# One decoder layer in one program: the mLSTM denominators, with blocks of scores and weighted queries added on VectorE ahead of the product with the ones column

## The chip, the core and the metric

The kernel runs on one core of one Trainium2 chip. The metric is the device time of one execution in microseconds. Three runs of the kernel before gave 2320.81, 2321.09 and 2322.24 us; the median is 2321.09 us.

## What is computed

One layer of a hybrid decoder for 256 prompt tokens and 8 x 8 sample tokens, 320 tokens in all, in fp32. An input projection feeds two token mixers, an mLSTM (4 heads, key width 256, value width 512) and an HGRN2 (8 heads); their outputs are gated, projected, normalised, and followed by a feed-forward part. The change touches only the denominator of the mLSTM:

```python
        s = jnp.einsum('bhtk,bhsk->bhts', qc, kc) * d
        num = jnp.einsum('bhts,bhsv->bhtv', s, vc) + w_inter[..., None] * jnp.einsum('bhtk,bhkv->bhtv', qc, C)
        den = jnp.sum(s, axis=-1) + w_inter * jnp.einsum('bhtk,bhk->bht', qc, n)
        h = num / jnp.maximum(jnp.abs(den), jnp.exp(-m_t))[..., None]
```

`den` is, for each token, the sum of its row of scores, and for sample tokens also the weighted query times the normaliser state `n`.

## The kernel before

**Main products.** TensorE multiplies the 320 tokens by one 128-column tile of weights after another (`run_main`, lines 499 to 534). Each weight is held as a high and a low part in a rounded fp32 format (`wh`, `wl`, later `bb`), each activation as well (`xh`, `xl`), so that each 128 x 128 block takes three products: high by high, high by low, low by high. These are the rows with 128x320 on line 348, the helper through which nearly all products go. A weight half-tile (a unit, 128x1024) is loaded by a DMA into `wr` (line 496), ScalarE writes its high part (line 486, shown as line 342, ScalarE's helper), and VectorE subtracts to get the low part (line 488).

**Side work.** All else (mixers, gates, norms) is written as Python generators that a planner (`Sched`, lines 144 to 242) runs while the main products are emitted. After every block of three main products the planner is pumped: a generator's next operation is emitted if, by the planner's own estimate of each engine's time, its inputs will be ready by then. TensorE operations must by that estimate be ready 450 units of time (nanoseconds of the planner) ahead, and only some 900 units of them fit between two blocks. The result is one fixed order of instructions for each engine, with semaphore waits between engines.

**The mLSTM heads.** For each head `m_S` (line 905) makes scores: three blocks of score products are multiplied by decay factors into the tile `E`. Columns 0 to 127 are prompt tokens 0 to 127 against keys 0 to 127, columns 128 to 255 are tokens 128 to 255 against keys 0 to 127, columns 256 to 383 are tokens 128 to 255 against keys 128 to 255, and columns 384 to 511 (partitions 64 to 127) the sample tokens. ScalarE and VectorE then split `E` into high and low parts (lines 925 to 929) for the numerator's products. `m_num` (line 1056) makes numerators and denominators of the prompt tokens: a block of `E` as the stationary operand times a column of ones (`one`, in the tile `misc`) gives row sums in a PSUM bank (lines 1069 to 1071: one product for the first tile of tokens, two that accumulate for the second). `m_sample` (line 1128) does the sample tokens: it writes the weighted queries times `n` into two blocks of the tile `qn` (line 1141), and takes three accumulating products with the ones column, one with the sample block of `E` and two with `qn` (lines 1159 to 1161). Line 1163 copies the sum out of PSUM on VectorE.

So each head has six products with the ones column, 24 in all. In the profile they are the rows `bank<-misc,f` 128x1; being plain fp32, each is two passes, so the profile counts 48 and its timeline shows each as x2.

`E`, `qn` and the weighted queries are parts of the tiles that the profile calls `f`; `ra` are the rounded parts for numerators.

Of the kernel before, what the change touches and what calls it, by code (L numbers as in the profile page):

```python
# [13 lines left out]
ALU = mybir.AluOpType  # L14
# [230 lines left out]
def wait(*evs):  # L245
    return ("wait", evs)


def acq(pool, n=1):
    return ("acq", pool, n)  # L250
# [6 lines left out]
def post(ev):  # L257
    return ("set", ev)


def act(n, psum=False, ptr=0):
    return ((61 if psum else 112) + n) / 1.2 + 93 * ptr


def dve(n, psum=False, mode=1, ptr=0):
    return ((62 if psum else 66) + n / mode) / 0.96 + 55 * ptr
# [6 lines left out]
def pe_r(n):  # L273
    return max(108.0, n * 0.425)
# [8 lines left out]
def cap(ap, off, dims):  # L283
    return bass.AP(ap.tensor, ap.offset + off, [list(ap.ap[0])] + [list(x) for x in dims])


def by_row(ap, off, gap):

    return cap(ap, off, [[32, 4], [8, 2], [1, 8]] if gap else [[8, 4], [32, 2], [1, 8]])


def by_token(ap, off, gap):

    return cap(ap, off, [[8, 2], [32, 4], [1, 8]] if gap else [[32, 2], [8, 4], [1, 8]])
# [11 lines left out]
class Program:  # L306
# [598 lines left out]
    def m_S(self, h):  # L905
        v, m = self.nc.vector, self.mh[h]
        if h:
            yield wait(self.mh[h - 1]["S"])
        yield wait(*m["q"], *m["k"], m["E"])
        b = yield acq(self.sbank)  # L910
        qk = m["qk"]
        for lo, n, ks, qs in ((0, 256, 0, lambda c: qk[:, c, 0:256]), (256, 128, 128, lambda c: qk[:, c, 128:256]),
                              (384, 64, 192, lambda c: by_row(qk[:, c, :], 256, False))):
            for c in range(2):
                yield ("pe", pe_f(n), lambda: self.mm(
                    b[:, lo:lo + n], qk[:, 2 + c, ks:ks + 128], qs(c), start=c == 0, stop=c == 1))
        E, Es = m["eb"], m["Es"]
        yield ("dve", dve(384, True), lambda: v.tensor_tensor(E[:, 0:384], b[:, 0:384], E[:, 0:384], ALU.mult))
        yield ("dve", dve(64, True), lambda: v.tensor_tensor(Es, b[64:128, 384:448].rearrange("p (x r) -> p x r", x=4), Es, ALU.mult))
        yield rel(self.sbank, b)  # L920
        shl = yield acq(self.shl)
        m["shl"] = shl
        sh, sl, ss = shl
        f = lambda x: x.bitcast(F32)
        yield ("act", act(384), lambda: self.A(sh, E[:, 0:384]))
        yield ("act", act(128), lambda: self.A(ss[64:128, 0:128], E[64:128, 384:512]))
        yield ("dve", dve(384), lambda: v.tensor_tensor(sl, E[:, 0:384], f(sh), ALU.subtract))
        yield ("dve", dve(128), lambda: v.tensor_tensor(ss[64:128, 128:256], E[64:128, 384:512], f(ss[64:128, 0:128]), ALU.subtract))
        yield ("act", act(256), lambda: self.A(ss[0:64], f(ss[64:128])))
        yield post(m["S"])  # L930

    def m_V(self, h):
# [123 lines left out]
    def m_num(self, h):  # L1056
        v, m = self.nc.vector, self.mh[h]
        if h:
            yield wait(self.mh[h - 1]["N"])
        yield wait(m["S"], m["Vt"])  # L1060
        hb = yield acq(self.hb)
        m["hb"] = hb
        E = m["eb"]
        sh, sl, ss = m["shl"]
        vh, vl = m["vhl"][:, 0], m["vhl"][:, 1]
        db = yield acq(self.sbank)
        m["db"] = db
        one = self.one
        yield ("pe", 212, lambda: self.mm(db[:, 0:1], E[:, 0:128], one, start=True, stop=True))
        yield ("pe", 212, lambda: self.mm(db[:, 1:2], E[:, 128:256], one, start=True, stop=False))  # L1070
        yield ("pe", 212, lambda: self.mm(db[:, 1:2], E[:, 256:384], one, start=False, stop=True))
        for i in range(2):
            b = yield acq(self.sbank)
            jobs = [(c, s) for c, s in (((0, 0),), ((128, 0), (256, 1)))[i]]
            n = 0
            for c, s in jobs:
                for x, w in ((sh, vh), (sh, vl), (sl, vh)):
                    st, sp = n == 0, n == 3 * len(jobs) - 1
                    yield ("pe", pe_r(512), lambda: self.mm(b, x[:, c:c + 128], w[:, s, :], start=st, stop=sp))
                    n += 1  # L1080
            yield from self.ln_post(h, i, b, db[:, i:i + 1], hb[:, i, :], 128, True)
            yield rel(self.sbank, b)
        yield rel(self.sbank, db)
        yield post(m["N"])
# [43 lines left out]
    def m_sample(self, h):  # L1128
        nc, v, m = self.nc, self.nc.vector, self.mh[h]
        if h:  # L1130
            yield wait(self.mh[h - 1]["QW"])
        yield wait(*m["q"], m["bc_"], self.rows_ev)
        qk, bc = m["qk"], m["bc"]

        qz = yield acq(self.qz)
        qn = yield acq(self.qn)
        for c in range(2):
            qc = cap(qz, 256 * c, [[136, 2], [32, 4], [1, 8]])
            yield ("dve", dve(64), lambda: v.tensor_tensor(qc, by_token(qk[:, c, :], 256, False), by_token(bc, 640, False), ALU.mult))
            n4 = cap(self.n0[:, h, c, :], 0, [[4, 2], [1, 4], [0, 8]])  # L1140
            yield ("dve", dve(64), lambda: v.tensor_tensor(by_token(qn, 128 * c, True), qc, n4, ALU.mult))
        yield post(m["QW"])
        nb = yield acq(self.sbank)
        for k in range(2):
            yield wait(*m["parts"][8 * k:8 * k + 8])
            cbs = m["cbs"][8 * k:8 * k + 8]
            yield ("pe", PE_C, lambda: [self.mm(
                nb[32 * x:32 * x + 32, :], qz[:, 256 * c + 128 * k + 32 * x:256 * c + 128 * k + 32 * x + 32], cbs[4 * c + x],
                start=k == 0 and c == 0, stop=False, skip_group_check=True) for c in range(2) for x in range(4)])
            for c in range(2):  # L1150
                self.s.spawn(self.m_update(h, 8 * k + 4 * c, cbs[4 * c:4 * c + 4]), 3)
        yield rel(self.qz, qz)
        yield wait(m["S"], m["Vt"])
        E = m["eb"]
        ss = m["shl"][2]
        for i in range(2):
            yield ("pe", pe_r(512), lambda: self.mm(nb, ss[:, 128 * i:128 * i + 128], m["vs"], start=False, stop=i == 1, skip_group_check=True))
        db = yield acq(self.sbank)
        yield ("pe", 212, lambda: self.mm(db[:, 0:1], E[:, 384:512], self.one, start=True, stop=False))
        for c in range(2):  # L1160
            yield ("pe", 212, lambda: self.mm(db[:, 0:1], qn[:, 128 * c:128 * c + 128], self.one, start=False, stop=c == 1))
        dn = yield acq(self.sm)
        yield ("dve", 80, lambda: v.tensor_copy(dn[:, 0:1], db[:, 0:1]))
        yield rel(self.sbank, db)
        yield rel(self.qn, qn)
        yield post(m["S0"])
        yield wait(m["N"])
        hb = m["hb"]
        yield from self.ln_post(h, 2, nb, dn[:, 0:1], hb[:, 2, :], 128, True)
        yield rel(self.sbank, nb)  # L1170
        yield rel(self.sm, dn)
        for j in range(4):
            b = yield acq(self.sbank)
            for i in range(3):
                yield ("pe", PE_T, lambda: nc.tensor.transpose(b[:, 128 * i:128 * i + 128], hb[:, i, 128 * j:128 * j + 128], self.ident))  # L1175
            jj = 4 * h + j
            o = yield acq(self.tst)
            g = self.vec[:, V_MLG + jj:V_MLG + jj + 1]
            yield ("act", act(NP_, True, 1), lambda: self.A(o[:, 0:NP_], b[:, 0:NP_], scale=g))
            yield ("act", act(64, True, 1), lambda: self.A(by_row(o, NP_, False), by_row(b, NP_, True), scale=g))  # L1180
            yield rel(self.sbank, b)
            yield ("sp", 620, lambda: self.dma(self.hT[jj], o))
            yield post(self.hT_ev[jj])
            yield wait(self.later())
            yield rel(self.tst, o)
        yield rel(self.hb, hb)
        yield wait(*m["inter"])
        yield rel(self.bc, bc)
        yield wait(m["KS"])
        yield post(m["end"])  # L1190
        if h == MH - 1:
            yield ("sp", 620, lambda: self.dma(self.d["n_out"][:, 0:8], self.np_o))
            yield ("sp", 620, lambda: self.dma(self.d["n_out"][:, 8:72], self.nso_flat))
# [857 lines left out]
```

## Time and profile before

The profiled execution took 2321.41 us by the clock that gives the three times above; its trace spans 2319.6 us, so 1.8 us lie around the span.

| what | from the page or the trace |
|---|---|
| median of three runs | 2321.09 us |
| profiled execution / its span | 2321.41 / 2319.6 us |
| TensorE (PE) busy | 2309.1 us, 15808 products |
| VectorE (DVE) busy | 1351.6 us |
| ScalarE (ACT) busy | 1059.5 us |
| granted TensorE clock | 0.999 of full |
| first and last product with the ones column | 100.0 and 364.2 us |

A busy share counts every engine's time, whether anybody waits for it or not. A product's duration in the trace is longer than the distance between two starts, because products are pipelined: what one costs is read from the starts of its neighbours.

### The profile page before, as it was taken

To read this page: it belongs to the slowest core of one execution; us is meant where nothing else is said; L and a number is where in the kernel's file an instruction comes from. 1 tells how busy PE (TensorE), PEld (TensorE's weight loads), DVE (VectorE), ACT (ScalarE), POOL (GpSimd) and SP (SyncE) were. 2 spreads that over 40 slices of the span, in tenths; PEclk is the share of its full clock that TensorE was granted. 3 is DMA by queue.
4 is the path that set the end of the run, shared out by engine and by line. 5 is a ranking of instruction groups with operands and counts; after the bars stand their busy time and mean duration, and the time that the engine had idled before them with its cause. 6 is when DMAs were issued, how large, how long until landed. Compare 5 with 4: busy or idle time off the path is not lost.

```text
span 2319.6 us, 38982 instructions
## 1 busy us (share of the span) xinstructions
PE 2309.1 (100%) x15808; PEld 2267.0 (98%) x15808; DVE 1351.6 (58%) x2297; ACT 1059.5 (46%) x1703; POOL 11.9 (1%) x37
## 2 busy tenths in 40 slices
PE   9999999999999999999999999999999999999998
PEld 9999999999999999999999999999999999999997
DVE  6566567666666776555555767654444444444455
ACT  5444445555556565444433446533442343234333
POOL 0000000000000000000000000000000000000000
PEclk9999999999999999999999999999999999999999
DMA  7676777555555555555545654444444444444465
GB/s 282 206 254 223 269 280 230 193 187 181 183 181 188 182 189 172 174 177 169 176 169 176 213 167 152 150 146 154 146 155 146 154 147 154 146 153 147 153 219 182
DMA packets 143275, 424.92 MB, mean 183 GB/s; under 512 B 16372, under 2 KB 37748, under 8 KB 142072
## 3 DMA queue, kind: packets, MB, share of 16 engines
q1 hardware_dynamic: 141800, 415.96, 53.9%
q0 software_dynamic: 1152, 6.29, 0.8%
q8 instruction: 123, 2.02, 0.4%
q14 instruction: 56, 0.46, 0.1%
q10 hardware_dynamic: 144, 0.20, 0.0%
HBM read 371.48 MB, written 50.90 MB: 182 GB/s over the span
## 4 chain that ended last, share of the span: by engine, by line
PE 98%; ACT 1%; DVE 0%; DMA 0%; issue 0%; SPq 0%; ACTq 0%; DVEq 0%
PE bank L348 97%; ACT f3m L342 0%; DMA f<-first 0%; PE bank L1610 0%; PE bank L946 0%; PE bank L1175 0%; PE bank L1448 0%; DVE f3m L1938 0%; ACT f L342 0%; PE bank L1453 0%; PE bank L1019 0%; PE bank L1502 0%; PE bank L993 0%; PE bank L1559 0%; ACT oC L342 0%
## 5 line engine op out<-in xcount | busy, mean ns | idle before, releaser
L348 PE MATMUL bank<-xh,wh 128*128 128x320 f32 (+1 forms) x2432 | 782.4, 322 | 0.3 <-ACT wh L342 0.3
L488 DVE TENSOR_TENSOR wl<-wr,wh 128x1024 fp32r<-128x1024 f32 x426 | 522.0, 1225 | 399.6 <-ACT wh L342 395.9
L348 PE MATMUL bank<-xh,wl 128*128 128x320 f32 (+1 forms) x2432 | 752.2, 310 | 0.0
L348 PE MATMUL bank<-xl,wh 128*128 128x320 f32 (+1 forms) x2432 | 749.8, 309 | 0.0
L342 ACT ACTIVATE wh<-wr 128x1024 fp32r<-128x1024 f32 x426 | 451.0, 1059 | 498.1 <-PE bank L348 478.2
L348 PEld LDWEIGHTS bank<-xh,wh 128*128 128x128 f32 x2432 | 457.8, 188 | 19.2 <-issue 14.7
L348 PEld LDWEIGHTS bank<-xl,wh 128*128 128x128 f32 x2432 | 458.1, 189 | 2.9
L348 PEld LDWEIGHTS bank<-xh,wl 128*128 128x128 f32 x2432 | 458.0, 188 | 0.5 <-DVE wl L701 0.3
L488 DVE TENSOR_TENSOR bb<-wr,bb 128x1024 fp32r<-128x1024 f32 x176 | 215.7, 1226 | 229.2 <-ACT bb L342 229.1
L342 ACT ACTIVATE bb<-wr 128x1024 fp32r<-128x1024 f32 x176 | 186.4, 1059 | 313.3 <-PE bank L348 294.9
L348 PE MATMUL bank<-xh,bb 128*128 128x320 f32 (+1 forms) x1280 | 285.4, 309 | 0.0
L348 PE MATMUL bank<-rxb,bb 128*128 128x320 f32 x1208 | 276.3, 309 | 0.0
L348 PE MATMUL bank<-ra,wh 128*128 128x320 f32 x988 | 265.9, 308 | 0.0
L348 PE MATMUL bank<-ra,bb 128*128 128x320 f32 x1096 | 264.2, 308 | 0.7 <-DVE ra L1640 0.7
L348 PEld LDWEIGHTS bank<-xh,bb 128*128 128x128 f32 x1280 | 215.0, 188 | 0.0
L348 PEld LDWEIGHTS bank<-rxb,bb 128*128 128x128 f32 x1208 | 204.3, 188 | 0.2
L348 PE MATMUL bank<-xl,bb 128*128 128x320 f32 (+1 forms) x640 | 197.7, 309 | 0.0
L348 PEld LDWEIGHTS bank<-ra,bb 128*128 128x128 f32 x1096 | 187.1, 188 | 1.2 <-DVE ra L1640 0.9
L348 PEld LDWEIGHTS bank<-ra,wh 128*128 128x128 f32 x988 | 176.3, 188 | 0.0
L348 PE MATMUL bank<-rxb,wh 128*128 128x320 f32 x548 | 169.0, 308 | 0.0
L348 PE MATMUL bank<-rxb,wl 128*128 128x320 f32 x548 | 169.0, 308 | 0.0
L348 PEld LDWEIGHTS bank<-xl,bb 128*128 128x128 f32 x640 | 120.4, 188 | 0.3 <-DVE xl L1863 0.3
(263 smaller groups left out, 2233.9 us busy)
## 6 DMA issues: line engine op xcount, KB each, us to landing
wr<-wt SPq DMA_DIRECT2D x602, 512.0 KB, 3.4
rx<-C SPq DMA_DIRECT2D x34, 256.0 KB, 5.6
Cs<-rx SPq DMA_DIRECT2D x34, 256.0 KB, 4.4
f<-C SPq DMA_DIRECT2D x30, 256.0 KB, 5.3
Cs<-f SPq DMA_DIRECT2D x30, 256.0 KB, 4.8
f<-first SPq DMA_DIRECT2D x6, 704.0 KB, 10.8
vD<-ra SPq DMA_DIRECT2D x4, 1024.0 KB, 6.8
f<-S SPq DMA_DIRECT2D x8, 512.0 KB, 6.6
```

Of the source, the lines that this page charges most:

```text
L342: return self.nc.scalar.activation(out, in_, func, **kw)
L348: self.nc.tensor.matmul(*a, **kw)
L488: self.V().tensor_tensor(lo, raw, hi.bitcast(F32), ALU.subtract)
```

## The change

Three additions on VectorE take the place of three of the six products in each head:

- at the end of `m_S`: the second block of `E` for tokens 128 to 255 is added to the first (128x128), after both have been split; `m_num` then takes one product for that tile of tokens where it took two;
- in `m_sample`, after the weighted queries: the second block of `qn` is added to the first (128x128);
- in `m_sample`, just ahead of the product: the sample block of `E` is added to the lower half of `qn` (64x128), and one product is left of three.

```diff
@@ m_S
         yield ("act", act(256), lambda: self.A(ss[0:64], f(ss[64:128])))
+        yield ("dve", dve(128), lambda: v.tensor_tensor(E[:, 256:384], E[:, 256:384], E[:, 128:256], ALU.add))
         yield post(m["S"])
@@ m_num
         yield ("pe", 212, lambda: self.mm(db[:, 0:1], E[:, 0:128], one, start=True, stop=True))
-        yield ("pe", 212, lambda: self.mm(db[:, 1:2], E[:, 128:256], one, start=True, stop=False))
-        yield ("pe", 212, lambda: self.mm(db[:, 1:2], E[:, 256:384], one, start=False, stop=True))
+        yield ("pe", 212, lambda: self.mm(db[:, 1:2], E[:, 256:384], one, start=True, stop=True))
@@ m_sample
+        yield ("dve", dve(128), lambda: v.tensor_tensor(qn[:, 0:128], qn[:, 0:128], qn[:, 128:256], ALU.add))
         yield post(m["QW"])
...
+        yield ("dve", dve(128), lambda: v.tensor_tensor(qn[64:128, 0:128], qn[64:128, 0:128], E[64:128, 384:512], ALU.add))
         db = yield acq(self.sbank)
-        yield ("pe", 212, lambda: self.mm(db[:, 0:1], E[:, 384:512], self.one, start=True, stop=False))
-        for c in range(2):
-            yield ("pe", 212, lambda: self.mm(db[:, 0:1], qn[:, 128 * c:128 * c + 128], self.one, start=False, stop=c == 1))
+        yield ("pe", 212, lambda: self.mm(db[:, 0:1], qn[:, 0:128], self.one, start=True, stop=True))
```

In the whole program TensorE's list of instructions is 12 rows shorter (24 products with the ones column become 12) and VectorE's 12 rows longer. Because the planner places all side work, other side products, stores and loads near the four heads also move to other slots; TensorE's list is the same again from about 443 us of the span on, but for the numbers of lines and buffers.

On TensorE, in the sample part of the first head, the kernel before has a product with the ones column (`misc`) in the slots between blocks of main products (`xh`, `xl`, `wh`, `wl`), in turn with products of the numerator (`ra`); this is the first to the second of the three:

```order
L348 MATMUL bank_82<-xh,wl 128x320
L348 MATMUL bank_86<-misc,f_76 128x1
L348 MATMUL bank_82<-xh,wh 128x320
L348 MATMUL bank_82<-xl,wh 128x320
L348 MATMUL bank_82<-xh,wl 128x320
L348 MATMUL bank_84<-ra 128x512
L348 MATMUL bank_82<-xh,wh 128x320
L348 MATMUL bank_82<-xl,wh 128x320
L348 MATMUL bank_82<-xh,wl 128x320
L348 MATMUL bank_86<-misc,f_76 128x1
```

With the change there is one such product at that place, about where the third was:

```order
L348 MATMUL bank_82<-xh,wl 128x320
L348 MATMUL bank_84<-ra 128x512
L348 MATMUL bank_86<-misc,f_76 128x1
L348 MATMUL bank_82<-xh,wh 128x320
L348 MATMUL bank_82<-xl,wh 128x320
```

It now follows a numerator product in the same slot; the two slots that held the other two are left to main products and numerators.

On VectorE, at the same place, the kernel before ends the normalisation of a tile (lines 1054 and 1041), splits a unit of weights (line 488), and then copies the sample denominator (line 1163):

```order
L1054 TENSOR_TENSOR misc<-misc 128x1
L1041 TENSOR_SCALAR f_77<-f_77,misc 128x512
L488 TENSOR_TENSOR wl<-wr,wh 128x1024
L1163 COPY misc<-bank_86 128x1
L488 TENSOR_TENSOR wl<-wr,wh 128x1024
```

With the change (lines 1055 and 1042 are the old 1054 and 1041) the addition on the new line 1159 stands between the split and the copy:

```order
L1055 TENSOR_TENSOR misc<-misc 128x1
L1042 TENSOR_SCALAR f_77<-f_77,misc 128x512
L488 TENSOR_TENSOR wl<-wr,wh 128x1024
L1159 TENSOR_TENSOR f_76<-f_76 64x128
L1163 COPY misc<-bank_86 128x1
L488 TENSOR_TENSOR wl<-wr,wh 128x1024
```

The product now waits for that addition, and the copy for the product.

## The prediction

> **What bounds the kernel now.** I read the page's busy times and its chain first, then the list of what TensorE waited for, then the stretches of the span in which the four mLSTM heads run.
>
> ```profile
> span 2319.6 us, 38982 instructions
> PE 2309.1 (100%) x15808; PEld 2267.0 (98%) x15808; DVE 1351.6 (58%) x2297; ACT 1059.5 (46%) x1703; POOL 11.9 (1%) x37
> PE 98%; ACT 1%; DVE 0%; DMA 0%; issue 0%; SPq 0%; ACTq 0%; DVEq 0%
> ```
>
> The chain that ends last is TensorE for 98% of the span. A busy TensorE need not be one that nobody holds up, so the next view lists all of its waits:
>
> ```profile
> PE bank L348 <- POOL ones L631: 1.0, 1, 1.0
> PE bank L348 <- DVE ra L1640: 0.7, 1, 0.7
> PE bank L348 <- ACT wh L342: 0.3, 1, 0.3
> ```
>
> Three waits, 2.0 us together in 2319.6 us. And by stretches (columns: TensorE, its weight loads, VectorE, ScalarE, GpSimd busy, clock, DMA share, GB/s), one for each of the four heads:
>
> ```profile
> 90.00:165.00 75.00, 75.00 (x517) 70.83 (x517) 47.04 (x97) 31.39 (x51) 0.00 (x0) 1.00 0.71 239
> 165.00:252.00 87.00, 87.00 (x598) 79.06 (x598) 52.76 (x103) 38.47 (x68) 0.00 (x0) 1.00 0.76 263
> 252.00:338.00 86.00, 86.00 (x594) 80.02 (x594) 52.67 (x104) 39.53 (x69) 0.00 (x0) 1.00 0.75 265
> 338.00:385.00 47.00, 47.00 (x321) 44.03 (x320) 33.59 (x68) 23.95 (x39) 0.00 (x0) 1.00 0.60 195
> ```
>
> TensorE is busy in every microsecond of them at full clock (1.00). VectorE is busy 47 of 75, 53 of 87, 53 of 86 and 34 of 47 us. So in these stretches the end is set by how long TensorE's own list takes: a product taken off it is time gained, and an addition on VectorE costs nothing as long as nobody comes to wait for it.
>
> **What twelve products are worth.** The group of products with the ones column, and their weight loads:
>
> ```profile
> L348 PE MATMUL bank<-misc,f 128*128 128x1 f32 x48 | 6.7, 208 | 0.0
> L348 PEld LDWEIGHTS bank<-misc,f 128*128 128x128 f32 x48 | 8.1, 189 | 0.0
> ```
>
> 48 passes are 24 products, of 6.7 / 24 = 0.28 us busy each; with pipelined products that is only an upper bound. What one costs is seen in the starts around it. The first one, and then the third of the sample part of the first head with the split and the copy on VectorE before and after it:
>
> ```profile
> 99.67 0.31 PE L348 MATMUL bank<-xl,wh 128*128 128x320 f32 x1
> ...
> 99.82 0.31 PE L348 MATMUL bank<-xh,wl 128*128 128x320 f32 x1
> 99.82 0.33 PEld L348 LDWEIGHTS bank<-misc,f 128*128 128x128 f32 x2
> 99.96 0.28 PE L348 MATMUL bank<-misc,f 128*128 128x1 f32 x2
> ...
> 100.10 0.39 PE L348 MATMUL bank<-xh,wh 128*128 128x320 f32 x1
> ...
> 100.33 0.31 PE L348 MATMUL bank<-xl,wh 128*128 128x320 f32 x1
> ```
>
> ```profile
> 114.89 0.28 PE L348 MATMUL bank<-misc,f 128*128 128x1 f32 x2
> ...
> 115.16 1.23 DVE L488 TENSOR_TENSOR wl<-wr,wh 128x1024 fp32r<-128x1024 f32 x1 [3.17 <-ACT wh L342]
> ...
> 116.22 0.28 PE L348 MATMUL bank<-misc,f 128*128 128x1 f32 x2
> ...
> 117.41 0.32 PE L348 MATMUL bank<-xh,wl 128*128 128x320 f32 x1
> ...
> 117.56 0.28 PE L348 MATMUL bank<-misc,f 128*128 128x1 f32 x2
> ...
> 117.70 0.39 PE L348 MATMUL bank<-xh,wh 128*128 128x320 f32 x1
> ...
> 117.88 0.16 DVE L1163 COPY misc<-bank 128x1 f32<-128x1 f32 x1 [1.49 <-PE bank L348]
> 117.93 0.30 PE L348 MATMUL bank<-xl,wh 128*128 128x320 f32 x1
> ```
>
> The plain step of a main product comes from the longest piece of the chain:
>
> ```profile
> 1509.15 784.96 PE bank L348 x5344
> ```
>
> 784.96 / 5344 = 0.147 us. In the first place it is 100.33 - 99.82 = 0.51 us from the main product ahead of the one with the ones column to the second one behind it, in the other 117.93 - 117.41 = 0.52 us. Without it two steps, 0.294 us, would lie between. So one product costs 0.515 - 0.294 = **0.22 us**: 0.14 us up to the next start, and 0.08 us because that next main product takes 0.23 us to its successor instead of 0.147.
>
> Three products go in each of four heads: 12 x 0.22 = **2.64 us**. The bounds: below, the 0.14 us of the slot alone, 12 x 0.14 = 1.7 us; above, the busy time, 12 x 0.28 = 3.4 us. I take 0.22, which is what two places show.
>
> Here a rule of the Trainium skill speaks against the size of the gain. The page "TensorE: Matmul & The Clock Gate" (section "Back-to-back issue gap") gives a matmul with up to 64 columns a floor of about 25 ns; for two passes that would be 0.05 us a product and 0.6 us for twelve. The same page (section "LDWEIGHTS (loading the stationary operand)") gives a weight load its columns over 1.2 GHz, 107 ns for 128: two loads are 0.21 us and twelve products 2.6 us. The trace sides with the loads: 0.22 us measured, for one column that streams.
>
> **What the additions cost.** 128x128 in fp32 from SBUF to SBUF has a row of its own, and 64x128 too:
>
> ```profile
> L1378 DVE TENSOR_TENSOR f<-f 128x128 f32<-128x128 f32 x30 | 8.5, 285 | 0.0
> L928 DVE TENSOR_TENSOR ra<-f,ra 64x128 fp32r<-64x128 f32 x4 | 1.2, 290 | 0.1
> L1163 DVE COPY misc<-bank 128x1 f32<-128x1 f32 x4 | 0.6, 158 | 5.6 <-PE bank L348 5.6
> ```
>
> Eight of 0.285 and four of 0.29 us are 3.4 us of VectorE, about 0.9 us a head, in stretches where it idles 13 to 34 us. Their inputs are VectorE's own results, or tiles that ScalarE has long read when the instruction ahead of the addition (lines 927, 928) starts, so I see no new wait on VectorE for the first two additions of a head. The third, on line 1159, stands just ahead of the copy on line 1163, ahead of which VectorE now idles for 5.6 us in four times, waiting for TensorE: the addition fits in there. What is queued behind that copy is the next split of weights. Its cover is the lead of the splits:
>
> ```profile
> ACT wh L342 <- PE bank L348: 53.7, 30, 3.8
> ...
> ACT wh L342 <- DMA wr<-wt: 2.2, 1, 2.2
> ```
>
> (waits of ScalarE between 60 and 420 us). Where ScalarE waits ahead of a conversion of weights, it is nearly always for TensorE to give a buffer back, 53.7 us in 30 waits, and for a load once, 2.2 us. Splits are as far ahead as the three buffers let them be, and TensorE waited for none of them in these stretches. Some 0.3 us more on VectorE three times a head uses up a small part of that lead. If the cover were gone, each addition would cost its 0.29 us, 3.4 us in all, more than the gain.
>
> **The wait that is added.** The two products that are left now need an addition that has just been issued. The tighter case is the sample part. In the first head the split ahead of the addition ends at 115.16 + 1.23 = 116.39 us, the addition at about 116.7. TensorE reached the product at 117.56; it stays at about that place in the list, and three products ahead of it in this head are gone, so it comes there at 117.56 - 0.66 = 116.9 us. That leaves 0.2 us. In TensorE's queue the next main products stand behind that product, so a late addition would be paid in full. I count nothing, and up to 0.3 us in this head for the bound.
>
> **What moves.** Near the heads, transposes and state products change slots, and stores of states, of head outputs and of gates change places among the weight loads in SyncE's list; the number of transfers is the same, and GpSimd's list is untouched. From 443 us on TensorE's list is as before. A side product costs what it costs in any slot; only where two come to stand side by side, or are parted, is one 0.08 us gained or lost. With half a dozen such places that is at most 0.5 us either way; I take 0.
>
> **The sum.** The profiled execution took 2321.41 us with a span of 2319.6. 2321.41 - 2.64 = 2318.8 us for that execution. It lies 0.3 us above the median of the three runs, 2321.09; from the median it is 2318.45. I forecast **2318.5 us**, 0.11% less.
>
> **The rivals.** A measurement of this kernel can tell about 0.2% (4.6 us) from no change.
>
> *TensorE waits for the additions (slower).* If an addition ends only after TensorE has come to its product, everything behind it stands still. The price at each of the eight products is at most one split and one addition, 1.23 + 0.29 = 1.5 us, 12.2 us in all; less the gain, 2321.1 + 12.2 - 2.6 = 2330.6 us. It decides where the 0.2 us above turn negative. For it: the planner's order is fixed by estimates, and the new product is placed close behind its addition. Against it: the split itself waits for ScalarE, which waits for TensorE, so it comes earlier as TensorE does, and TensorE's list of waits shows not one on VectorE in the heads. Chance 0.04, of which 0.03 above 2325.7.
>
> *Only the slot is gained.* If the 0.08 us behind each product is owed to the slot between two blocks and not to the product, and the slots stay in use by other side work, 12 x 0.14 = 1.7 us: 2319.4 us. The floor of 25 ns that the page "TensorE: Matmul & The Clock Gate" of the Trainium skill states would lead further that way, to 0.6 us and 2320.5. Against it: the third place above is bracketed by main products alone and shows the 0.52 us whole. Chance 0.10.
>
> *More than the products.* The denominators come a block or two earlier, side products close up, and the upper price holds: 3.4 + 0.5 = 3.9 us, 2317.2 us. Chance 0.09, of which 0.05 for still more, beyond 4.6 us, which would take a hidden wait that no view here shows.
>
> *A load comes late.* The stores that move in SyncE's list hold up a weight load by the 2.2 us that one already waited, and it reaches TensorE: 2318.5 + 2.2 = 2320.7 us. Chance 0.04, of which 0.02 for several such and a time beyond 2325.7.
>
> That the change doesn't do what it says is no rival: the order of instructions has 12 products with the ones column where there were 24.
>
> **How the numbers follow.** The forecast has 0.73. The range reaches from the upper price with some 0.6 us of spread between runs, 2316.6, to the late load, 2320.7; it leaves out the waits on additions and the far gains. Faster by over 0.2%: 0.05. Slower by over 0.2%: 0.03 + 0.02 = 0.05. Within 0.2%: 0.90.
>
> **What would show it.** The group with the ones column counts 24 passes and about 3.4 us busy; TensorE's busy time falls by some 2.6 us to about 2306.5 and the span to about 2317. The new lines on VectorE show 0.28 to 0.29 us each. In the sample part, one product with 0.51 us from the main product ahead to the second one behind, and the copy on line 1163 waiting less than 5.6 us. The forecast is wrong if TensorE's list of waits shows VectorE's lines 930 or 1159, or if the span falls by less than 1.7 us with no wait in that list.

## The result and the profile after

The changed kernel takes 2317.85 us (median of 20 runs, 2317.22 to 2318.62), against 2321.10 us (20 runs, 2320.28 to 2322.24): 3.25 us less, a ratio of 0.9986 (95% interval 0.9980 to 0.9992). The forecast was 2318.5 us, 2.6 us less; the interval of the ratio reaches from 1.9 to 4.6 us less. The profiled execution took 2318.6 us.

The page, in the order in which the prediction read that of before:

```profile
span 2316.8 us, 38947 instructions
PE 2307.3 (100%) x15784; PEld 2265.5 (98%) x15784; DVE 1353.7 (58%) x2309; ACT 1059.0 (46%) x1703; POOL 12.0 (1%) x37
PE 99%; ACT 1%; DVE 0%; issue 0%; ACTq 0%; POOL 0%; DVEq 0%; POOLq 0%
```

The span fell by 2.8 us, TensorE's busy time by 1.8. TensorE has 24 passes fewer, VectorE 12 instructions more and 2.1 us more to do. All waits of TensorE in the span:

```profile
PE bank L348 <- POOL ones L631: 1.0, 1, 1.0
PE bank L348 <- DVE ra L1640: 0.7, 1, 0.7
```

No wait for an addition is among them; both were there before. The stretches of the four heads (columns as in the prediction):

```profile
90.00:165.00 75.00, 75.00 (x517) 70.85 (x516) 48.40 (x100) 31.81 (x52) 0.00 (x0) 1.00 0.71 239
165.00:252.00 87.00, 87.00 (x595) 78.80 (x594) 53.91 (x108) 38.22 (x68) 0.00 (x0) 1.00 0.78 265
252.00:338.00 86.00, 86.00 (x593) 80.01 (x593) 53.06 (x106) 40.44 (x70) 0.00 (x0) 1.00 0.78 267
338.00:385.00 47.00, 47.00 (x318) 44.04 (x317) 32.03 (x66) 24.20 (x39) 0.00 (x0) 1.00 0.55 182
```

TensorE is still busy in every microsecond of them, at full clock. The group that lost half of its products (last columns: busy, mean ns, idle time ahead and who ended it):

```profile
L348 PE MATMUL bank<-misc,f 128*128 128x1 f32 x24 | 3.3, 208 | 0.0
L348 PEld LDWEIGHTS bank<-misc,f 128*128 128x128 f32 x24 | 4.1, 189 | 0.1
```

VectorE's lines:

```profile
L1142 DVE TENSOR_TENSOR f<-f 128x128 f32<-128x128 f32 x4 | 1.2, 292 | 0.1
L1159 DVE TENSOR_TENSOR f<-f 64x128 f32<-64x128 f32 x4 | 1.2, 290 | 0.1
...
L930 DVE TENSOR_TENSOR f<-f 128x128 f32<-128x128 f32 x4 | 1.2, 288 | 0.1
...
L1163 DVE COPY misc<-bank 128x1 f32<-128x1 f32 x4 | 0.6, 157 | 3.8 <-PE bank L348 3.8
```

The three additions show 0.292, 0.290 and 0.288 us, and the copy behind the one on line 1159 still has 3.8 of the 5.6 us of idle time ahead of it. The sample part of the first head, which the prediction took for the tightest place:

```profile
116.19 0.29 DVE L1159 TENSOR_TENSOR f<-f 64x128 f32<-64x128 f32 x1
...
116.74 0.31 PE L348 MATMUL bank<-xh,wl 128*128 128x320 f32 x1
...
116.89 0.40 PE L348 MATMUL bank<-ra 128*128 128x512 f32 x1
...
117.12 0.28 PE L348 MATMUL bank<-misc,f 128*128 128x1 f32 x2
...
117.26 0.39 PE L348 MATMUL bank<-xh,wh 128*128 128x320 f32 x1
...
117.43 0.16 DVE L1163 COPY misc<-bank 128x1 f32<-128x1 f32 x1 [0.96 <-PE bank L348]
117.49 0.31 PE L348 MATMUL bank<-xl,wh 128*128 128x320 f32 x1
```

The addition ends at 116.48 us. The product with the ones column starts at 117.12 us, 0.64 us later. It starts 0.23 us behind the numerator product, and the next main product 0.14 us behind it. The kernel before has the same 0.23 us at its one product of this kind that follows a numerator product (361.5 us), so there is no gap for the addition. Of the eight products that need an addition, the one in the sample part of the fourth head comes soonest behind it:

```profile
360.93 0.29 DVE L1159 TENSOR_TENSOR f<-f 64x128 f32<-64x128 f32 x1
...
361.78 0.28 PE L348 MATMUL bank<-misc,f 128*128 128x1 f32 x2
```

That is 0.56 us from the end of the addition to the start of the product. The other six have 1.1 us or more.

So the gain is there, and a little larger than forecast. Three readings of it were open. By the theory of the prediction, 12 products at 0.22 us are the whole of it, and the additions and the new order are worth nothing. By a first rival, the removed products are worth only their slot or less, and the planner's new order brought the rest. By a second, the additions cost something that a still larger gain covers.

### The profile page after: what moved, and what is told of

It reads as the page before. It is cut to its first block, busy times and chain, and to the rows that moved or that the text cites. A ratio compares the mean times of both kernels' runs of the same rounds, so it can differ in the third digit from the quotient of the medians.

```text
span 2316.8 us, 38947 instructions
## 1 busy us (share of the span) xinstructions
PE 2307.3 (100%) x15784; PEld 2265.5 (98%) x15784; DVE 1353.7 (58%) x2309; ACT 1059.0 (46%) x1703; POOL 12.0 (1%) x37
## 4 chain that ended last, share of the span: by engine, by line
PE 99%; ACT 1%; DVE 0%; issue 0%; ACTq 0%; POOL 0%; DVEq 0%; POOLq 0%
PE bank L348 97%; ACT f3m L342 0%; PE bank L1610 0%; PE bank L947 0%; PE bank L1175 0%; PE bank L1448 0%; DVE f3m L1938 0%; ACT f L342 0%; PE bank L1453 0%; PE bank L1020 0%; PE bank L1502 0%; PE bank L994 0%; PE bank L1559 0%; ACT oC L342 0%; ACT oS L342 0%
```

## How the experiments are read

Each kernel ran beside the kernel before on the same chip; ratios are against those runs. The intervals reach some 2 us either way, as far as most of the effects, so the medians alone settle little, and the traces are read in three pieces as well. Main products are the same in all of these kernels, in the same order, so the start of the 201st and of the 2401st main product (near 40 and 429 us) enclose the four heads everywhere. Behind the 2401st, up to the last main product, every trace takes 1862.8 us. The third piece is the tail from the last two stores to the end of the span.

One thing had to be taken off first, and no list of waits shows it. Twice in each head TensorE takes eight products with memory states (line 1148 of the changed kernel) in a row, 16 passes in the profile, with loaded states (`f`, `rx`) as inputs. In the changed kernel the timeline of TensorE has the fourth such group as follows (columns: start, us, then the instruction):

```profile
192.00 1.06 PE L348 MATMUL bank<-rx,f 128*32 128x512 f32 x8
192.88 1.85 PE L348 MATMUL bank<-f 128*32 128x512 f32 x8
194.66 0.41 PE L348 MATMUL bank<-xh,wh 128*128 128x320 f32 x1
```

And in `noadds`, an experiment below with the same order but without the additions:

```profile
191.06 1.07 PE L348 MATMUL bank<-rx,f 128*32 128x512 f32 x8
191.95 1.08 PE L348 MATMUL bank<-f 128*32 128x512 f32 x8
192.96 0.41 PE L348 MATMUL bank<-xh,wh 128*128 128x320 f32 x1
```

From the start of the group to the next main product it is 194.66 - 192.00 = 2.66 us in the first and 192.96 - 191.06 = 1.90 in the second; most groups take 1.85. The 0.8 us lie between products whose times overlap, so TensorE counts as busy and no wait is listed. What comes late is a state's load. SyncE's stores of updated states and the loads that reuse their buffers, in the changed kernel:

```profile
181.08 1.41 SPq L351 DMA_DIRECT2D Cs<-f  x3
...
185.45 0.33 SPq L351 DMA_DIRECT2D Cs<-f  x1
...
188.17 1.65 SPq L351 DMA_DIRECT2D f<-C  x3
...
191.31 0.33 SPq L351 DMA_DIRECT2D f<-C  x1
```

The first load goes out as the first store lands (188.16 us). The load that the group waits for is the second of these three. Here it is alone, in the changed kernel:

```profile
188.87 0.34 SPq L351 DMA_DIRECT2D f<-C  x1
```

And in `noadds`:

```profile
187.96 0.34 SPq L351 DMA_DIRECT2D f<-C  x1
```

By its semaphore it lands at 193.64 us in the first, 4.77 us after its issue, and the last product of the group that waits starts 0.04 us later, at 193.68. In `noadds` it lands at 191.94 us, after 3.98 us. It leaves 3.1 us ahead of the start of the group in both, so the 0.8 us are the longer time of the transfer. (The load that stands alone at 191.31 us lands at 196.18 us, when the group is over.)

In the kernel before the third group had such a wait of 0.60 us (165.79 to 168.24 us). In most of the other traces it is the fourth group, with additions and without: 0.00 to 0.94 us. It differs from one execution to the next, as the load takes 3.7 to 5.1 us. It also depends on how far ahead of the group the load leaves: 3.8 us in both traces of the kernel before, 3.1 in both of the changed one, 2.7 and 3.0 in the two of `skip12` below. So part of it may belong to the changed order, and taking it off prices the products alone, not the whole change. In the table it is taken off before a product is priced against 388.90 us, which both traces of the kernel before leave (389.50 - 0.60, and 389.22 - 0.32).

| kernel | median us (runs) | ratio, 95% interval | span | heads | late loads | rest against 388.90 | per product |
|---|---|---|---|---|---|---|---|
| changed | 2317.85 (20) | 0.9986, 0.9980 to 0.9992 | 2316.8 | 387.10 | 0.81 | -2.61 | 0.22 |
| `skip12` | 2319.04 (11) | 0.9991, 0.9982 to 1.0000 | 2316.8 | 387.05 | 0.86 | -2.71 | 0.23 |
| `noadds` | 2318.39 (11) | 0.9988, 0.9979 to 0.9997 | 2315.5 | 386.31 | 0.05 | -2.64 | 0.22 |
| `tile_part` | 2319.82 (11) | 0.9995, 0.9986 to 1.0004 | 2317.7 | 388.71 | 0.67 | -0.86 | 0.22 |
| `twice` | 2326.44 (10) | 1.0023, 1.0014 to 1.0032 | 2324.7 | 394.36 | 0 | +5.46 | 0.23 |
| `before_again` | 2321.22 (11) | 0.9999, 0.9990 to 1.0008 | 2319.4 | 389.22 | 0.32 | 0.00 | |
| `after_again` | 2317.24 (11) | 0.9983, 0.9974 to 0.9992 | 2315.9 | 386.93 | 0.61 | -2.58 | 0.22 |
| `skip12_again` | 2318.86 (11) | 0.9989, 0.9981 to 0.9998 | 2316.8 | 387.17 | 0.94 | -2.67 | 0.22 |
| `after_early` | 2317.35 (11) | 0.9983, 0.9974 to 0.9992 | 2315.6 | 386.17 | 0 | -2.73 | 0.23 |
| `thin` | 2326.90 (8) | 1.0025, 1.0015 to 1.0036 | 2324.6 | 394.91 | 0 | +6.01 | 0.25 |
| `pool1` | 2320.64 (11) | 0.9998, 0.9989 to 1.0007 | 2319.2 | 389.15 | 0.24 | +0.01 | |

(The kernel before had 2321.08 us beside the first four experiments, 2321.29 beside the next four and 2320.94 beside the last two. "Per product" divides by the number of products taken away or added: 12, 12, 12, 4, 24, 12, 12, 12, 24.)

## The experiments

**skip12: the products gone, nothing else changed.** On the kernel before:

```diff
-        yield ("pe", 212, lambda: self.mm(db[:, 1:2], E[:, 128:256], one, start=True, stop=False))
-        yield ("pe", 212, lambda: self.mm(db[:, 1:2], E[:, 256:384], one, start=False, stop=True))
+        yield ("pe", 212, lambda: None)
+        yield ("pe", 212, lambda: self.mm(db[:, 1:2], E[:, 256:384], one, start=True, stop=True))
...
-        yield ("pe", 212, lambda: self.mm(db[:, 0:1], E[:, 384:512], self.one, start=True, stop=False))
+        yield ("pe", 212, lambda: None)
         for c in range(2):
-            yield ("pe", 212, lambda: self.mm(db[:, 0:1], qn[:, 128 * c:128 * c + 128], self.one, start=False, stop=c == 1))
+            yield ("pe", 212, lambda: c and self.mm(db[:, 0:1], qn[:, 128:256], self.one, start=True, stop=True))
```

> The order of the kernel before, word for word, with the same twelve products taken off TensorE's list and nothing added, so that no side work changes its slot. The denominators lack one block of scores, the sample tokens' scores and one block of weighted queries. If a product is worth 0.22 us and the new order nothing: 12 x 0.22 = 2.6 us less than before, 2318.5 us. If only the slot of 0.14 us is saved and the rest of the 3.25 us comes from the new order: 1.7 us less, 2319.4 us. If the whole gain of the change lies in the products (0.27 us each): 3.25 us less, 2317.85 us.

Measured: 2319.04 us, 2.0 us less than its kernel before. That lies between the first two readings (2.6 and 1.7 us), and the time alone does not choose. In the heads the trace is 2.71 us shorter once late loads are taken off. The products alone are worth what the prediction gave them; the new order is not needed for it.

**noadds: the new order without the additions.** On the changed kernel, lines 930, 1142 and 1159:

```diff
-        yield ("dve", dve(128), lambda: v.tensor_tensor(E[:, 256:384], E[:, 256:384], E[:, 128:256], ALU.add))
+        yield ("dve", dve(128), lambda: None)
...
-        yield ("dve", dve(128), lambda: v.tensor_tensor(qn[:, 0:128], qn[:, 0:128], qn[:, 128:256], ALU.add))
+        yield ("dve", dve(128), lambda: None)
...
-        yield ("dve", dve(128), lambda: v.tensor_tensor(qn[64:128, 0:128], qn[64:128, 0:128], E[64:128, 384:512], ALU.add))
+        yield ("dve", dve(128), lambda: None)
```

> The order of the changed kernel, with its twelve additions on VectorE not issued while the planner still counts them; all else is in the same place. The denominators lack the blocks that would have been added. If the additions are hidden: the time of the changed kernel, 2317.85 us, within 0.3 us. If TensorE pays for them, by waits or by later splits: up to 12 x 0.29 = 3.4 us less than the changed kernel, 2314.4 us.

Measured: 2318.39 us, 2.7 us less than its kernel before, where the changed kernel gained 3.25. Leaving the additions out gains nothing. The heads give -2.64 us against -2.61 with the additions, and at all twelve products with the ones column the step from the product ahead is the same in both traces within 0.01 us. The additions cost nothing at the products that need them; the rival that they cost something falls. Only whether they make the late load later is not told by one trace (0.05 us here, 0.81 and 0.61 with them); `skip12` has 0.86 and 0.94 without any addition. The profiled span is 1.3 us shorter than that of the changed kernel, but 0.76 us of that is the late load and 0.94 us the start (below), less 0.40 us in the tail: none of it lies where the additions are.

**twice: each product issued two times in its slot.** On the kernel before:

```diff
-        yield ("pe", 212, lambda: self.mm(db[:, 0:1], E[:, 0:128], one, start=True, stop=True))
+        yield ("pe", 212, lambda: [self.mm(db[:, 0:1], E[:, 0:128], one, start=x == 0, stop=x == 1) for x in range(2)])
...
-        yield ("pe", 212, lambda: self.mm(db[:, 0:1], E[:, 384:512], self.one, start=True, stop=False))
+        yield ("pe", 212, lambda: [self.mm(db[:, 0:1], E[:, 384:512], self.one, start=x == 0, stop=False) for x in range(2)])
...
```

(the other four of a head likewise)

> The order of the kernel before, with each of the 24 products with the ones column issued twice in a row in its slot (the denominators come out doubled). If 0.14 us is the product's own and 0.08 us is paid once for the slot: 24 x 0.14 = 3.4 us more than before, 2324.5 us. If each product costs 0.22 us wherever it stands: 5.3 us more, 2326.4 us. If a product costs only the floor of its two passes, some 0.05 us: 1.2 us more, 2322.3 us.

Measured: 2326.44 us, 5.4 us more. The first place, which read 0.51 us with one product:

```profile
99.94 0.31 PE L348 MATMUL bank<-xh,wl 128*128 128x320 f32 x1
99.94 0.56 PEld L348 LDWEIGHTS bank<-misc,f 128*128 128x128 f32 x4
100.09 0.50 PE L348 MATMUL bank<-misc,f 128*128 128x1 f32 x4
...
100.45 0.39 PE L348 MATMUL bank<-xh,wh 128*128 128x320 f32 x1
...
100.68 0.31 PE L348 MATMUL bank<-xl,wh 128*128 128x320 f32 x1
```

From 99.94 to 100.68 us it is 0.74 us: the second product adds 0.23 us, as much as the first. All 24 added ones come to 5.46 / 24 = 0.23 us. The price belongs to the product. Were 0.08 us of it owed to the slot, the second one would have cost 0.14.

**tile_part: only the part of `m_S` and `m_num`.** The changes of the diff in these two functions alone, on the kernel before:

```diff
+        yield ("dve", dve(128), lambda: v.tensor_tensor(E[:, 256:384], E[:, 256:384], E[:, 128:256], ALU.add))
...
-        yield ("pe", 212, lambda: self.mm(db[:, 1:2], E[:, 128:256], one, start=True, stop=False))
-        yield ("pe", 212, lambda: self.mm(db[:, 1:2], E[:, 256:384], one, start=False, stop=True))
+        yield ("pe", 212, lambda: self.mm(db[:, 1:2], E[:, 256:384], one, start=True, stop=True))
```

> Only the part in m_S and m_num: one addition and one product less in each head, with the planner's own new order. At 0.22 us a product and an order worth nothing: 0.9 us less than before, 2320.2 us. If the new order is what gives more than 2.6 us in the whole change, a part with an order of its own may be off that by 0.5 us either way: 2319.7 to 2320.7 us.

Measured: 2319.82 us, 1.3 us less; the interval of the ratio takes in 1. The heads give -0.86 us, 0.22 for each of the four products. Its tail is shorter too, like that of the changed kernel, which is where the median's other 0.4 us can come from.

**before_again, after_again, skip12_again.** The three programs without an edit, on one chip.

> The kernel before once more, unchanged, as a measure of what two sets of runs of one program differ by, and for a second trace. If sets of ten runs agree: within 0.2 us of 2321.1 us. If the time of a build or a set wanders by half a microsecond, as the first experiments against their traces would have it: up to 0.6 us either way. In the trace, the eight groups of state products of the mLSTM heads (1.85 us each where no load is late): if late state loads come and go between executions, another group than the third is longer, or none; if they belong to the order, again the third by 0.6 us.

> The changed kernel once more, unchanged. If its gain is the twelve products at 0.226 us and the rest scatter: some 2.7 us less than before, 2318.4 us, within 0.5. If the 3.25 us are a property of the order: 2317.85 us again, within 0.2. In the trace, the same question for the fourth group of state products, 0.81 us longer in the first trace.

> The order of the kernel before without the twelve products, once more (the same part of the denominators is left out). If the first result (2.0 us less than before) was scatter: nearer to 2.7 us less, 2318.4 us. If late state loads in this order take 0.7 us on average: 2.0 us less again, 2319.05 us, and the fourth group of state products is late again.

Measured: 2321.22, 2317.24 and 2318.86 us. The kernel before repeats within 0.2 us, and its late load is in another group (the fourth, 0.32 us). The changed kernel is 4.05 us faster than the kernel before beside it (2321.29 us), where the first set gave 3.25; that is more than either reading of it expected. `skip12` gains 2.4 us here and 2.0 in the first set. In these sets the changed kernel is 1.6 us faster than `skip12`; the first sets gave 1.2 us. In the heads the two differ by 0.24 us in this pair of traces, no more than their late loads do (0.94 against 0.61); of what is left the tail, 0.7 us, is the part that repeats. The rest of the 1.2 and 1.6 us has no cause here.

The tail is read from the last two stores and SyncE's last waits (for the stores to land, and for the engines at the end of the program). In the kernel before, its waits (us in total, times, longest) and the row of the stores in its timeline:

```profile
SPq L2047 <- DMA Sp<-oS: 2.6, 1, 2.6
...
SPq L2047 <- PEq L2047: 1.0, 2, 0.5
```

The stores:

```profile
2314.22 0.98 SPq L351 DMA_DIRECT2D Sp<-oS  x2
```

In the changed kernel, the same two views:

```profile
SPq L2047 <- DMA Sp<-oS: 2.4, 1, 2.4
...
SPq L2047 <- PEq L2047: 0.7, 2, 0.5
```

The stores:

```profile
2312.07 0.96 SPq L351 DMA_DIRECT2D Sp<-oS  x2
```

From the stores to the end of the span it is 2319.6 - 2314.22 = 5.38 us before and 2316.8 - 2312.07 = 4.73 us after: 0.65 us less, in instructions that the change does not touch. The same difference is 5.37 to 5.54 us in all traces with the order of before (`skip12` and `twice` among them) and 4.66 to 4.79 in `after_again`, `tile_part` and `after_early`.

**after_early: the states' updates earlier.** On the changed kernel, to have the loads and stores of the fourth group together:

```diff
-        s.spawn(self.m_states(h), 3)
+        s.spawn(self.m_states(h), 1)
```

> The changed kernel with the loads of the mLSTM states given a higher rank in the planner (1 where it was 3), so that they go ahead of weight loads and stores in SyncE's list where both are ready; the four loads of the fourth group then stand together. If TensorE loses 0.6 to 0.8 us to late state loads in most executions: all eight groups take 1.85 us, and the time is 0.6 us less than the changed kernel, 2317.2 us. If those waits are rare, or if the order of side work moves as much: within 0.4 us of the changed kernel, 2317.5 to 2318.3 us.

Measured: 2317.35 us, against 2317.24 for the unedited one beside it: no difference. In the trace the four stores and the four loads do go out together and no group waits for a load, and the heads are 0.76 us shorter than in `after_again`; the median does not follow. The edit was aimed at the load that stood alone, and the one that is late is the second of the others; here it leaves 3.4 us ahead of the group and takes 3.69 us, the shortest of all traces, so that this trace has no wait may be chance. That the late load holds TensorE up is shown where it occurs; how often it occurs in executions without a profile stays open.

**thin: small products added.** On the kernel before, 24 more products with a block of 32 columns in place of 128 as the stationary operand, into a column that nothing reads; two of the six lines of a head:

```diff
-        yield ("pe", 212, lambda: self.mm(db[:, 0:1], E[:, 0:128], one, start=True, stop=True))
+        yield ("pe", 212, lambda: [self.mm(db[:, 0:1], E[:, 0:128], one, start=True, stop=True), self.mm(db[0:32, 4:5], E[:, 0:32], one, start=True, stop=True), self.mm(db[0:32, 4:5], E[:, 32:64], one, start=True, stop=True)])
...
-        yield ("pe", 212, lambda: self.mm(db[:, 0:1], E[:, 384:512], self.one, start=True, stop=False))
+        yield ("pe", 212, lambda: [self.mm(db[0:32, 4:5], E[:, 384:416], self.one, start=True, stop=True), self.mm(db[:, 0:1], E[:, 384:512], self.one, start=True, stop=False)])
...
```

> The order of the kernel before, and with the products with the ones column 24 more in the same slots, each with only 32 of the 128 columns of the block as the stationary operand; they write a column that nobody reads. They stream one column like the others. If the weight loads, by their columns, set the price: about a quarter of 0.22 us, 24 x 0.06 = 1.4 us more than before, 2322.6 us. If each product has its price whatever it loads: 24 x 0.225 = 5.4 us more, 2326.6 us.

Measured: 2326.90 us, 6.0 us more, above both readings (1.4 and 5.4 us). The first two places:

```profile
99.28 0.31 PE L348 MATMUL bank<-xh,wl 128*128 128x320 f32 x1
99.43 0.49 PE L348 MATMUL bank<-misc,f 128*128 128x1 f32 x6
99.85 0.41 PE L348 MATMUL bank<-xh,wh 128*128 128x320 f32 x1
100.10 0.31 PE L348 MATMUL bank<-xl,wh 128*128 128x320 f32 x1
...
100.69 0.31 PE L348 MATMUL bank<-xh,wl 128*128 128x320 f32 x1
100.93 0.54 PE L348 MATMUL bank<-misc,f 128*32 128x1 f32 x4
101.32 0.40 PE L348 MATMUL bank<-xh,wh 128*128 128x320 f32 x1
101.56 0.31 PE L348 MATMUL bank<-xl,wh 128*128 128x320 f32 x1
```

In the first, two thin products stand behind a full one: 100.10 - 99.28 = 0.82 us instead of 0.51, so 0.15 each. In the second, one stands ahead of a full one and adds 101.56 - 100.69 - 0.51 = 0.36 us. The four thin passes of the first place start 0.03 us apart, some 0.06 us a product, while the passes with the full block in `twice` start 0.11 us apart. One column streams in both, so the width of the block makes the difference. A price by columns of the weight load would have it so, but the output is narrower as well (32 rows for 128). The rest of the time is the change of width. The first thin pass comes 0.24 us behind a main product instead of 0.147, and steps back to full blocks are longer too: of the 0.31 and 0.36 us that the two places take more, the thin passes themselves account for 0.12 and 0.06, which leaves 0.2 and 0.3 us for going to the 32-column form and back. The Trainium skill, "TensorEngine Tiling (Array Packing)", section "Key Properties", says that changing the tiling mode drains TensorE; the trace shows the longer steps, but not whether they are a drain. As the change of width costs more than the thin products, the time of this run does not measure the load's share.

**pool1: one more GpSimd instruction.** The trace's list of GpSimd has 74 instructions in the kernel before and 75 in the changed one, semaphore steps counted. On the kernel before, one memset is repeated:

```diff
         nc.gpsimd.memset(self.eps, EPS)
+        nc.gpsimd.memset(self.eps, EPS)
```

> The kernel before with one instruction more in GpSimd's list, a repeated memset of one column at the start; all other lists are unchanged. In the traces so far the last semaphore steps of GpSimd take 0.4 us longer in all builds with the order of before than in those with the changed order, whose GpSimd list has one semaphore wait more. If the length of that list decides: the stretch from the end of SyncE's last wait to the end of the span falls from 1.21 to 0.82 us, and the time by 0.4 us, 2320.8 us. If it does not: 1.21 us, and 2321.2 us.

Measured: 2320.64 us, 0.30 us less, which its interval cannot tell from nothing. In the trace the last step does change. From the instruction behind SyncE's last wait for a transfer to the end of the span it is 1.21 or 1.22 us in every other trace with the order of before and 0.82 us here, as in every trace of the changed order; most of the difference is a stop of GpSimd between two of its last semaphore steps, 0.42 against 0.08 us. So 0.39 us of the tail hang on GpSimd's list and not on the additions; what makes GpSimd stop there is not shown. The other quarter microsecond, a shorter wait for the last stores, doesn't appear in `pool1` nor in `noadds` (5.18 and 5.17 us from the last two stores to the end) and has no cause here.

## Why the prediction was right, point by point

- **TensorE bounds the heads.** Shown: taking away work of TensorE alone (`skip12`) shortens them by 2.71 us and adding some (`twice`) lengthens them by 5.46, while 12 additions on VectorE (changed against `noadds`) make 0.03.
- **12 products at 0.22 us.** Shown in size: 0.22 to 0.23 us in eight traces. By the weight-load rule of the Trainium skill that the prediction quoted ("TensorE: Matmul & The Clock Gate", "LDWEIGHTS (loading the stationary operand)") two loads of 128 columns are 0.21 us, an estimate, and the trace agrees: the passes in `twice` start 0.11 us apart. By the floor of 25 ns that it quoted from the section "Back-to-back issue gap" of that page of the Trainium skill, `twice` would have added 1.2 us, an estimate too; it added 5.4.
- **The split into 0.14 and 0.08.** Not borne out. The longer step behind the product is part of the product's own price, for a second one in the same slot costs 0.23 us and not 0.14. The rival "only the slot is gained" falls with it, and so does the 0.08 us that the prediction gave or took for two such products side by side.
- **Additions hidden, 0.29 us each.** Shown by the rows (0.288 to 0.292 us) and by `noadds`.
- **The added wait at nothing.** Right, with more room than forecast. The prediction left 0.2 us in the first head and took it for the tightest place; the trace has 0.64 us there and 0.56 us in the fourth head. The addition ended at 116.48 us where 116.7 was forecast, and the product came at 117.12 instead of 116.9. TensorE's list has no wait for line 930 or 1159.
- **What moves, at nothing within 0.5 us.** Right in the heads, with late loads taken off: the new order gives -2.61 us, the old one without the products -2.71. But the prediction said that TensorE had three waits in all. It has a fourth kind, hidden in overlapping products, of up to 0.94 us. The rival "a load comes late" feared such a thing, but with 2.2 us and for a load of weights; it is a load of states, and a single profile can be off by the better part of a microsecond for it. The prediction also said that GpSimd's list is untouched: it has one semaphore wait more, and by `pool1` a list longer by one ends the program 0.39 us sooner.
- **The size.** The sum lacked one term: 0.65 us in the tail. 2.61 + 0.65 = 3.26 us meets the 3.25 of the medians, but so close a match is luck: late loads take back 0.25 us of it on average (0.81 and 0.61 us in the two traces of the changed kernel, 0.60 and 0.32 in those of the kernel before), and the second set of runs gave 4.05 us, 0.8 us more, for which there is no cause here.
- **The signs to look for.** 24 passes and 3.3 us came (3.4 forecast), and 2316.8 us of span (2317). The 0.51 us around a single product can be read in the fourth head, 0.52 us from 361.63 to 362.15; in the first head a numerator product stands between. Busy time fell by 1.8 us and not by 2.6: later loads (0.81 against 0.60 us) and a slower start count as busy and took back the rest. The span fell by more, 2.8 us, because the tail's 0.65 us and the wait of 0.3 us for line 342 (at 8 us of the span before, gone after) were not busy time.

## What to carry to other kernels

Where TensorE is the bound, price a small product from the starts of its neighbours: a product with a full block as the stationary operand and one streamed column cost 0.22 us here, more than a main product's 0.147, and an addition on an engine with idle time was a good exchange for it. For changes of a thousandth, compare traces piece by piece between instructions that both kernels have, since single spans of one program differ by a microsecond. And doubling a suspected cost in place tells its owner (slot or product) better than removing it does.

## What the runs showed that was not expected

- **Busy time can hide a wait.** Up to 0.9 us of waiting for a state's load lie in rows of products with no idle time between them; only the length of the group (2.66 against 1.85 us) tells.
- **Products of different widths.** Going from 128 to 32 columns and back cost TensorE 0.2 to 0.3 us together in `thin`.
- **The start.** The first main products step more slowly for a time that differs between executions. In the changed kernel's trace:

```profile
5.80 1.00 PE L348 MATMUL bank<-xl,wh 128*128 128x320 f32 x3
6.60 0.85 PE L348 MATMUL bank<-xh,wl 128*128 128x320 f32 x3
```

  In that of `noadds`, at the same time:

```profile
5.81 0.60 PE L348 MATMUL bank<-xh,wl 128*128 128x320 f32 x3
6.25 0.61 PE L348 MATMUL bank<-xh,wh 128*128 128x320 f32 x3
```

  Three products take 6.60 - 5.80 = 0.80 us in one and 6.25 - 5.81 = 0.44 in the other. The trace's record of the full granted clock begins at 7.1 us in the first and at 4.9 us in the second; that is not all of it, for in `twice` it begins at 4.9 us too and the 101st main product starts as late as 20.63 us. The 101st main product starts between 19.77 and 20.71 us in the traces of this study, with the same instructions ahead of it.
- **The end.** One more instruction in GpSimd's list took 0.39 us off the end of the program in the trace of `pool1`.
